# Block 1's feed forward: 28 of 32 inner tiles by seven half-size block products, the state space's tables kept in memory meanwhile

## The chip, the cores and the metric

The kernel runs on one core of a Trainium2 chip. TensorE (PE) does the matrix products; VectorE (DVE), ScalarE (ACT) and GpSimd (POOL) do everything element by element; SyncE (SP) issues most transfers between memory and the core. The metric is device time in microseconds, the median of several runs of the whole program.

## What is computed

Two transformer blocks over 512 tokens of 1024 features in float32. Block 1 is two attention mixers and a feed forward; block 2 is four mixers, one of them a state space (S5), and a gated feed forward. The change touches block 1's feed forward and the tables that block 2's state space reads:

```python
# block 1
hn = rms_norm(h, norm_mlp_pre)
ff = jnp.square(jax.nn.relu(hn @ w_ff1)) @ w_ff2     # 1024 -> 4096 -> 1024
h = h + rms_norm(ff, norm_mlp_post)
# block 2, the state space: these depend on parameters alone
mag = jnp.exp(lr * dt); ab_re = mag * jnp.cos(li * dt); ab_im = mag * jnp.sin(li * dt)
bb_re = cf_re[..., None] * bre - cf_im[..., None] * bim     # and bb_im
# block 2's feed forward
ff = (jax.nn.silu(a @ w_ffn_gate) * (a @ w_ffn_up)) @ w_ffn_down     # 1024 -> 2816 -> 1024
```

## The kernel before

**Products in three parts.** A float32 product is three reduced ones: each operand is split into a high and a low part, and `mm3` (L328 to L330) issues high x high, high x low and low x high into one PSUM bank. `wload` brings 128 x 1024 pieces of weights (`wraw`, three buffers), ScalarE casts the high part (`whi`, L308), VectorE subtracts to get the low part (`wlo`, L309); five buffers of each.

**Block 1's feed forward** (`ffn1`, L1361) makes 32 inner tiles of 128 features by 512 tokens. An inner tile takes 8 x 3 matmuls of 512 columns. `sink` then does relu and square on ScalarE, the square once more on GpSimd (L1375) and the low part on VectorE (L1376); the pair goes into the tag `hid`. `groups` (L1310) takes the tiles in groups of `FF1 = (6, 6, 6, 6, 4, 4)`. After a group's tiles and one tile of the next group (the lead), the group's share of the 4 x 2 outputs (token tile j, half f of the features) is formed in PSUM and added to a tile `y` in SBUF (`Post.part`, L606). The last group's share goes on into the norm (`Post.sink`, `Post.done`). The first five tiles (`HEAD`) of the first group run in half-width pieces (`layer`): three tiles and then two on the first 256 tokens, the two and then the three on the second 256, while the mixer's end still produces the second half of the input.

**The seven products.** Block 2's second matrix ("down") already takes four of its groups by seven products of half-size blocks in place of eight (`seven`, L1270). A group of four inner tiles is two pairs. `Pairs.pair` (L1252) forms, for a pair, two tiles of sums and differences on GpSimd (`sx` and `sy`, four operations of 128 x 256) and splits them, and the tiles themselves, into high and low (tag `g`, 14 buffers a group). `seven` loads four raw weight pieces (`wq`), forms four sums and differences of them on GpSimd (L1291 to L1296), splits seven operands and does seven products, each in two token halves of 2 x 3 matmuls. The products come in the order 1, 2, 7, 6, 4, 5, 3; only the first two need none of GpSimd's pair sums. Each result is added to one of 14 tiles (`Post.seven`, L624; copied the first time, L622). After the last such group `Post.joined` (L627) adds the tiles up to the outputs on GpSimd, 14 additions of 128 x 512.

**The state space's tables** depend on parameters alone and are made inside block 1's feed forward, between groups (the list `between`): `S5.scalars`, then for each half of the channels `S5.maps` in two steps (first many small GpSimd operations on 64 to 128 rows x 64 elements, then TensorE transposes and small products), then `S5.tables`. They fill 16 of the 18 buffers of tag `g` until block 2 reads them.

**Order.** Each engine runs its queue in order. The order in a queue is made when the program is built: by a planner that simulates the engines and takes, whenever an engine comes free, the first instruction in program order that is ready. `issue_after` keeps an instruction behind another of its own engine; `in_order` fixes TensorE's order in some stages.

Of the kernel before, what the change touches and what calls it, by code (L numbers as in the profile page):

```python
# [16 lines left out]
OP = mybir.AluOpType  # L17
# [6 lines left out]
NEG = -1e30  # L24
FF1 = (6, 6, 6, 6, 4, 4)
FF2 = (4, 4, 4, 4, 2, 4)
SEVEN = {"down": range(4)}

# [201 lines left out]
def program(ctx: ExitStack, tc: tile.TileContext, A, out):  # L230
# [227 lines left out]
    class Fill:  # L458


        def __init__(self, lag=1):
            self.plan, self.later = [], [None] * lag
# [765 lines left out]
    class Pairs:  # L1228
# [40 lines left out]

    def seven(nm, g, pairs, post):  # L1270

# [37 lines left out]

    def groups(sizes, tiles, xs, sink, carry, nm, hid, post, nxt, between=(), pairs=None):  # L1310

# [3 lines left out]
        for g, n in enumerate(sizes):  # L1315
            ms = list(range(n0, n0 + n))
            todo = [x for m in ms[lead:] for x in tiles(m)]
            layer(todo, lambda key: [key], xs, sink, first=0 if g else HEAD, carry=carry)
            lead = 1 if g + 1 < len(sizes) else 0
            layer([x for m in range(n0 + n, n0 + n + lead) for x in tiles(m)], lambda key: [key], xs, sink)  # L1320
            if g < len(between):
# [4 lines left out]
            if g in SEVEN.get(nm, ()):  # L1326
                seven(nm, g, pairs, post)
# [33 lines left out]
    def ffn1(carry, old, new, s5):  # L1361

        r2 = cp.tile([128, 4], F32, name="r2f")
        pre = carry[1]
        hid = {}

        def sink(key, ps, ts):
            m = key[1]
            if m not in hid:
                hid[m] = u("hidh", F32R, tag="hid"), u("hidl", F32R, tag="hid")  # L1370
            hi, lo = (t[:, ts] for t in hid[m])
# [6 lines left out]
        def stats():  # L1378
# [7 lines left out]

        po = Post("norm_mlp_post", old, new, "hid")
# [15 lines left out]
    class S5:  # L1403


        def scalars(self):
# [72 lines left out]
        def maps(self, hb):  # L1479
# [4 lines left out]
            VP = [u("vp", tag="s5") for _ in range(2)]  # L1484
            CP = [u("cp", tag="g") for _ in range(2)]
            C0 = u("c0", tag="s5")
# [26 lines left out]
            for c in range(2):  # L1513
                self.CP[c][hb] = CP[c]
            yield
            for c in range(2):
                tp = mps()
                for b in range(4):
                    PE.transpose(tp[:, 128 * b:128 * b + 128], VP[c][:, 128 * b:128 * b + 128], ident)
                self.VM[c][hb] = u("vm", tag="g")  # L1520
                (ACT.copy if c else DVE.tensor_copy)(self.VM[c][hb], tp)

# [17 lines left out]
            DVE.tensor_tensor(kv[:, :, 0:32], kv[:, :, 0:32], dd, op=OP.add)  # L1540
            self.TM[hb] = u("tmx", tag="g")
            POOL.memset(self.TM[hb], 0.0)
            tv = self.TM[hb].rearrange("p (b x) -> p b x", b=4)
            for i in range(4):
                (ACT.copy if i % 2 else DVE.tensor_copy)(tv[32 * i:32 * i + 32, :, 32 * i:128],
                                                         kv[:, :, 0:128 - 32 * i])

        def tables(self):
# [3 lines left out]
            for hb in range(2):  # L1552
                self.RH[hb] = u("rh", tag="g")
                for c in range(2):
                    self.CT[c][hb] = u("ct", tag="g")
                    POOL.memset(f(self.CT[c][hb])[:, :, 0:1], 1.0 - c)
                DVE.tensor_copy(f(self.RH[hb]), self.rho4[:, 4 * hb:4 * hb + 4, None].to_broadcast([128, 4, 128]))
                POOL.memset(f(self.RH[hb])[:, :, 0:1], 0.0)
            other = (self.nx(), self.nx())
            ts = [u("s5u", tag="s5") for _ in range(2)]  # L1560
            for s_ in range(7):
# [6 lines left out]
                if s_ < 6:  # L1568
                    cmul(*other, *cur, *cur, self.scr2, DVE)
                    cur, other = other, cur  # L1570

    def mix2(carry, old, new, s5):
# [800 lines left out]
```

## Time and profile before

| | us |
|---|---|
| median of 3 runs | 1507.68 (1506.07 to 1508.33) |
| the profiled execution | 1511.7 |
| its span, first to last instruction | 1510.0 |
| TensorE busy | 1464.1 (97%) |
| VectorE busy | 866.2 (57%) |
| ScalarE busy | 605.6 (40%) |
| GpSimd busy | 333.0 (22%) |

Block 1's feed forward lies at about 455 to 818 us, block 2's at about 1165 to 1505 us. A busy time is the time in which an engine works on some instruction; matmuls overlap, so TensorE's pace is read from the distance of their starts. In the row of a stretch the columns are: the stretch, its length, the busy time of PE, PEld (weight load), DVE, ACT and POOL with the number of instructions in brackets, the granted TensorE clock (1.00 is full), the busy share of the 16 DMA engines, and GB/s. A timeline row gives start, duration, engine, line, operation, output <- inputs, shape, count, and in square brackets how long the engine was idle before it and who ended that.

### The profile page before, as it was taken

The numbers are of one execution on the slowest core, as the hardware profiler recorded it, in microseconds if no ns is written. First come the engines' busy times: TensorE is split into PE (matmuls) and PEld (weight loads), VectorE is DVE, ScalarE is ACT, GpSimd is POOL, SyncE is SP. The second block draws the span as 40 slices with busy tenths as digits, with TensorE's granted clock in tenths as the row PEclk, the third lists the DMA queues.
The fourth block names the chain that finished last, engine by engine and source line by source line (L and its number), as shares of the span: only waits on it lengthen the run. The fifth ranks groups of instructions, "written<-read, shape, count | busy, mean of one in ns | idle before, by whom it ended". The sixth has DMA issues, their size and how long they took to land. (4 is left out here: it accounts for less than half of the span.)

```text
span 1510.0 us, 21333 instructions
## 1 busy us (share of the span) xinstructions
PE 1464.1 (97%) x8180; PEld 1217.4 (81%) x8184; DVE 866.2 (57%) x1641; ACT 605.6 (40%) x1131; POOL 333.0 (22%) x528
## 2 busy tenths in 40 slices
PE   8999999999999999999998999899998999999997
PEld 6888876688888888888887999667788888888885
DVE  5433368743746534334446686956646657586746
ACT  6344455533335342322325443543525453333322
POOL 0210110000201467203600052411000323134600
PEclk9999999999999999999999999978999999999999
DMA  8332121123234332322334424001115242341322
GB/s 294 117 112 79 57 65 43 43 84 98 96 103 150 119 112 61 122 84 84 112 99 137 150 87 118 30 29 42 43 58 194 84 143 81 98 129 39 139 85 84
DMA packets 54725, 147.32 MB, mean 98 GB/s; under 512 B 9824, under 2 KB 16368, under 8 KB 54624
## 3 DMA queue, kind: packets, MB, share of 16 engines
q1 hardware_dynamic: 52384, 143.38, 29.2%
q10 hardware_dynamic: 1776, 1.85, 0.4%
q8 instruction: 64, 1.05, 0.3%
q0 software_dynamic: 464, 0.74, 0.2%
q14 instruction: 37, 0.30, 0.1%
HBM read 135.12 MB, written 11.06 MB: 97 GB/s over the span
## 5 line engine op out<-in xcount | busy, mean ns | idle before, releaser
L308 ACT CAST whi<-wraw 128x1024 fp32r<-128x1024 f32 (+4 forms) x221 | 217.4, 989 | 381.2 <-PE acc L329 188.2
L309 DVE TENSOR_TENSOR wlo<-wraw,whi 128x1024 fp32r<-128x1024 f32 (+4 forms) x221 | 269.4, 1225 | 160.4 <-ACT whi L308 152.3
L328 PE MATMUL acc<-xh,whi 128*128 128x512 f32 (+1 forms) x920 | 347.9, 379 | 7.5 <-ACT whi L308 5.6
L330 PE MATMUL acc<-xh,wlo 128*128 128x512 f32 (+1 forms) x920 | 343.6, 374 | 1.9 <-DVE wlo L309 1.9
L329 PE MATMUL acc<-xl,whi 128*128 128x512 f32 (+1 forms) x920 | 344.1, 374 | 0.3 <-DVE xl L703 0.3
L328 PEld LDWEIGHTS acc<-xh,whi 128*128 128x128 f32 x920 | 174.2, 189 | 44.2 <-ACT whi L308 7.9
L330 PEld LDWEIGHTS acc<-xh,wlo 128*128 128x128 f32 x920 | 174.1, 189 | 33.8 <-DVE wlo L309 2.7
L329 PEld LDWEIGHTS acc<-xl,whi 128*128 128x128 f32 x920 | 174.3, 189 | 31.6 <-issue 1.0
L328 PE MATMUL acc<-whi,hidh 128*128 128x512 f32 x304 | 119.6, 395 | 0.0
L329 PE MATMUL acc<-wlo,hidh 128*128 128x512 f32 x304 | 119.2, 394 | 0.0
L330 PE MATMUL acc<-whi,hidl 128*128 128x512 f32 x304 | 118.9, 394 | 0.0
L328 PE MATMUL acc<-whi,xh 128*128 128x256 f32 (+3 forms) x352 | 114.5, 325 | 0.2 <-ACT mv L1902 0.2
L329 PE MATMUL acc<-wlo,xh 128*128 128x256 f32 (+3 forms) x352 | 111.7, 317 | 0.0
L330 PE MATMUL acc<-whi,xl 128*128 128x256 f32 (+3 forms) x352 | 111.6, 317 | 0.0
L1375 POOL TENSOR_TENSOR relu<-relu 128x512 f32<-128x512 f32 (+1 forms) x37 | 36.8, 1002 | 230.8 <-ACT hidh L1374 226.7
L328 PEld LDWEIGHTS acc<-whi,xh 128*128 128x128 f32 x352 | 68.3, 194 | 6.9 <-issue 2.2
L330 PEld LDWEIGHTS acc<-whi,xl 128*128 128x128 f32 x352 | 68.0, 193 | 3.9
L329 PEld LDWEIGHTS acc<-wlo,xh 128*128 128x128 f32 x352 | 68.2, 194 | 3.5
L329 PEld LDWEIGHTS acc<-wlo,hidh 128*128 128x128 f32 x304 | 57.2, 188 | 13.2
L330 PEld LDWEIGHTS acc<-whi,hidl 128*128 128x128 f32 x304 | 57.2, 188 | 13.2
L328 PEld LDWEIGHTS acc<-whi,hidh 128*128 128x128 f32 x304 | 57.2, 188 | 13.0
L1284 ACT CAST whi<-wq 128x1024 fp32r<-128x1024 f32 x28 | 29.5, 1055 | 62.1 <-PE acc L329 44.9
(582 smaller groups left out, 2572.0 us busy)
## 6 DMA issues: line engine op xcount, KB each, us to landing
wraw<-in_wp_dram SPq DMA_DIRECT2D x195, 512.0 KB, 3.6
wq<-in_wp_dram SPq DMA_DIRECT2D x16, 512.0 KB, 3.5
hd<-y SPq DMA_DIRECT2D x24, 256.0 KB, 4.4
hr<-hd SPq DMA_DIRECT2D x12, 512.0 KB, 4.5
hr<-in_xt_dram SPq DMA_DIRECT2D x8, 512.0 KB, 5.3
H<-in_xT_dram SPq DMA_DIRECT2D x8, 256.0 KB, 5.2
wraw<-in_wp_dram SPq DMA_DIRECT2D x16, 128.0 KB, 3.9
gain<-in_gv_dram SPq DMA_DIRECT2D x8, 256.0 KB, 4.4
```

The lines of the kernel that those rows point to most:

```text
L308: ACT.copy(hi[:, s], raw[:, s])
L309: eng.tensor_tensor(lo[:, s], raw[:, s], hi.bitcast(F32)[:, s], op=OP.subtract)
L328: PE.matmul(ps, lhsT=w[0], rhs=x[0], start=first, stop=False)
L329: PE.matmul(ps, lhsT=w[0], rhs=x[1], start=False, stop=False)
L330: PE.matmul(ps, lhsT=w[1], rhs=x[0], start=False, stop=last)
L1284: ACT.copy(hi, raw)
L1375: POOL.tensor_tensor(a, a, a, op=OP.mult)
```

## The change

Block 1's feed forward takes groups of four tiles, eight of them; the first seven reach the outputs by seven products. `sink` hands the squared tiles of these groups to `Pairs`; only the last group's four keep the old way. The sums and differences of the weight pieces run on VectorE here (`eng`), in block 2 still on GpSimd. The lead tile is formed in the same call of `layer` as the group, so the first five tiles are the first group and its lead. `sx` and `sy` get two buffers of their own. The buffers of tag `g` now hold the pairs' operands, so the state space's matrices and tables are built in tag `s5`, written to memory (`keep`) and read back into tag `g` by `load` in the last group. The steps of the state space are spread over the groups 0 to 5.

```diff
-FF1 = (6, 6, 6, 6, 4, 4)
+FF1 = (4,) * 8
-SEVEN = {"down": range(4)}
+SEVEN = {"ff2": range(7), "down": range(4)}
...
-            x, y = u("sx"), u("sy")
+            x, y = u("sx", tag="sx"), u("sy", tag="sx")
...
-            POOL.tensor_tensor(t, B1, t, op=OP.subtract)
+            eng.tensor_tensor(t, B1, t, op=OP.subtract)
             yield 7, parts(t)
-            POOL.tensor_tensor(t, t, A0, op=OP.add)
+            eng.tensor_tensor(t, t, A0, op=OP.add)
             yield 6, parts(t)
-            POOL.tensor_tensor(B0, B0, t, op=OP.subtract)
-            POOL.tensor_tensor(t, B1, t, op=OP.subtract)
+            eng.tensor_tensor(B0, B0, t, op=OP.subtract)
+            eng.tensor_tensor(t, B1, t, op=OP.subtract)
...
             todo = [x for m in ms[lead:] for x in tiles(m)]
+            lead = 1 if g + 1 < len(sizes) else 0
+            todo += [x for m in range(n0 + n, n0 + n + lead) for x in tiles(m)]
             layer(todo, lambda key: [key], xs, sink, first=0 if g else HEAD, carry=carry)
-            lead = 1 if g + 1 < len(sizes) else 0
-            layer([x for m in range(n0 + n, n0 + n + lead) for x in tiles(m)], lambda key: [key], xs, sink)
...
+            if m in pairs.of:
+                if m not in rel:
+                    rel[m] = u("relu")
+                a = rel[m][:, ts]
+                ACT.activation(a, ps, AF.Relu)
+                ACT.activation(a, a, AF.Square)
+                pairs.add(m, rel[m], ts)
+                return
...
-               [lambda: (stats(), step(maps[0])()), step(*maps), step(maps[1]), s5.tables])
+               [stats, step(maps[0]), step(maps[0]), step(maps[1]), step(maps[1]), s5.tables, lambda: None, s5.load],
+               pairs, DVE)
...
+        def keep(self, nm, c, hb, t):
+            d = self.kept[nm, c, hb] = dram.tile([128, 512], F32, name=f"k{nm}{c}{hb}")
+            nc.sync.dma_start(out=d, in_=t)
+        def load(self):
+            for hb in range(2):
+                for nm, to in (("vm", self.VM), ("ct", self.CT), ("rh", self.RH)):
+                    for c in range(2 if nm != "rh" else 1):
+                        self.back(nm, c, hb, to)
...
+        def back(self, nm, c, hb, to):
+            t = u(nm, tag="g")
+            nc.sync.dma_start(out=t, in_=self.kept[nm, c, hb])
...
-    with phase("f1", u=3, hid=14, s5=6):
+    with phase("f1", u=5, sx=2, s5=9):
...
-    with phase("f2", u=8):
+    with phase("f2", u=6, sx=2):
```

## Rows read from the trace of the kernel before

**Rows 1.** The page's first part: busy us of each engine.
```profile
PE 1464.1 (97%) x8180; PEld 1217.4 (81%) x8184; DVE 866.2 (57%) x1641; ACT 605.6 (40%) x1131; POOL 333.0 (22%) x528
```

**Rows 2.** Stretches, columns as told above: two of block 1, two of block 2.
```profile
780.00:800.00 20.00, 20.00 (x89) 16.46 (x88) 7.59 (x8) 8.31 (x11) 2.08 (x2) 1.00 0.33 107
820.00:840.00 20.00, 16.85 (x125) 15.00 (x122) 17.55 (x57) 11.74 (x28) 3.44 (x16) 1.00 0.74 243
1265.00:1285.00 20.00, 20.00 (x90) 16.57 (x89) 20.00 (x21) 8.53 (x11) 8.04 (x4) 1.00 0.48 147
```

**Rows 3.** Timeline of PE: end of half-width pieces; first and last of seven matmuls.
```profile
488.60 0.28 PE L330 MATMUL ops<-xh,wlo 128*128 128x256 f32 x1
...
1212.05 0.39 PE L330 MATMUL ops<-whi,prl 128*128 128x512 f32 x1
...
1213.41 0.39 PE L330 MATMUL ops<-whi,prl 128*128 128x512 f32 x1
```

**Rows 4.** Groups by line: count, busy us, mean ns, then idle us before them.
```profile
L309 DVE TENSOR_TENSOR wlo<-wraw,whi 128x1024 fp32r<-128x1024 f32 x195 | 255.2, 1311 | 155.4 <-ACT whi L308 147.3 <-PE mps L1519 5.0 <-DMA wraw<-in_wp_dram 0.8
...
L1285 DVE TENSOR_TENSOR wlo<-wq,whi 128x1024 fp32r<-128x1024 f32 x28 | 50.6, 1807 | 4.4 <-PE ops L330 2.4 <-ACT whi L1284 1.9
...
L624 DVE TENSOR_TENSOR y<-acc,y 128x512 f32<-128x512 f32 x24 | 15.4, 677 | 0.0
```

**Rows 5.** Timeline of DVE, from block 1's and block 2's feed forward.
```profile
583.99 1.23 DVE L309 TENSOR_TENSOR wlo<-wraw,whi 128x1024 fp32r<-128x1024 f32 x1 [1.79 <-ACT whi L308]
...
1360.79 0.69 DVE L2334 TENSOR_TENSOR sil<-sil,acc 128x512 f32<-128x512 f32 x1 [3.42 <-PE acc L330]
...
1366.62 0.69 DVE L336 TENSOR_TENSOR prl<-sy,prh 128x512 fp32r<-128x512 f32 x1
...
1373.65 0.42 DVE L1263 TENSOR_TENSOR a0l<-sil,a0h 128x256 fp32r<-128x256 f32 x1
...
1413.01 1.28 DVE L624 TENSOR_TENSOR y<-acc,y 128x512 f32<-128x512 f32 x2
```

**Rows 6.** Timeline of ACT, end of block 1's half-width pieces; one copy of block 2.
```profile
489.04 0.38 ACT L1373 ACTIVATE relu<-acc 128x256 f32<-128x256 f32 x1
...
491.74 1.04 ACT L1374 ACTIVATE hidh<-relu 128x256 fp32r<-128x256 f32 x3
...
1215.58 0.42 ACT L1262 CAST a0h<-sil 128x256 fp32r<-128x256 f32 x1
```

**Rows 7.** Timeline of POOL, first and last of a pair's four operations.
```profile
1361.55 0.74 POOL L1255 TENSOR_TENSOR sx<-sil 128x256 f32<-128x256 f32 x1 [14.41 <-DVE sil L2334]
...
1365.20 0.74 POOL L1258 TENSOR_TENSOR sy<-sil,sx 128x256 f32<-128x256 f32 x1
```

**Rows 8.** Timeline of POOL, second block of matrices and the tables, firsts and lasts.
```profile
569.01 0.29 POOL L1396 TENSOR_TENSOR s5t<-s5s,s5b 128x64 f32<-128x64 f32 x1
...
584.20 1.17 POOL L1396 TENSOR_TENSOR s5t<-s5s,s5b 128x64 f32<-128x64 f32 x1
...
605.50 0.54 POOL L1494 TENSOR_SCALAR cp<-s5t 64x64 f32<-64x64 f32 x2
...
707.47 0.14 POOL L1556 MEMSET ct<- 128x4 f32 x2
...
743.24 0.74 POOL L1401 TENSOR_TENSOR ct<-s5u 128x256 f32<-128x256 f32 x1
```

**Rows 9.** Timeline of POOL, inside the first block of matrices.
```profile
547.82 1.04 POOL L1375 TENSOR_TENSOR relu<-relu 128x512 f32<-128x512 f32 x1
548.82 0.29 POOL L1399 TENSOR_TENSOR s5t<-s5s,p 128x64 f32<-128x64 f32 x1
```

**Rows 10.** Timeline of POOL, first and last of the 14 additions.
```profile
1406.05 3.53 POOL L629 TENSOR_TENSOR hr<-hr,y 128x512 f32<-128x512 f32 x2 [9.36 <-DVE hr L624]
...
1428.94 1.31 POOL L629 TENSOR_TENSOR y<-y,p 128x512 f32<-128x512 f32 x1
```

**Rows 11.** DMA issues of the page: KB each, us to landing.
```profile
wraw<-in_wp_dram SPq DMA_DIRECT2D x195, 512.0 KB, 3.6
```

More of the change, by code (lines that the diff above doesn't have):

```diff
@@ L1268, in pair, with seven @@
             self.mark = self.mark or last(mybir.EngineType.Activation)
-    def seven(nm, g, pairs, post):
+    def seven(nm, g, pairs, post, eng):
         W = {}
@@ L1308, in seven, with groups @@
                 post.seven(g, i, j, ps)
-    def groups(sizes, tiles, xs, sink, carry, nm, hid, post, nxt, between=(), pairs=None):
+    def groups(sizes, tiles, xs, sink, carry, nm, hid, post, nxt, between=(), pairs=None,
+               eng=POOL):
         n0 = 0
@@ L1326, in groups @@
             if g in SEVEN.get(nm, ()):
-                seven(nm, g, pairs, post)
+                seven(nm, g, pairs, post, eng)
                 if g + 1 not in SEVEN[nm]:
@@ L1364, in ffn1 @@
         pre = carry[1]
-        hid = {}
+        hid, rel = {}, {}
         def sink(key, ps, ts):
             m = key[1]
+            if m in pairs.of:
[6 more added lines that the diff above has]
+                return
             if m not in hid:
-                hid[m] = u("hidh", F32R, tag="hid"), u("hidl", F32R, tag="hid")
+                hid[m] = u("hidh", F32R, tag="g"), u("hidl", F32R, tag="g")
             hi, lo = (t[:, ts] for t in hid[m])
@@ L1385, in ffn1 @@
         step = lambda *ms: lambda: [next(m, None) for m in ms]
-        po = Post("norm_mlp_post", old, new, "hid")
+        po, pairs = Post("norm_mlp_post", old, new, "u"), Pairs("ff2", FF1)
         nxt = Pre("ln_mix_pre_2")
         groups(FF1, lambda m: [("ff1", m)], pre.xs, sink, carry, "ff2", hid, po, nxt,
-               [lambda: (stats(), step(maps[0])()), step(*maps), step(maps[1]), s5.tables])
+               [stats, step(maps[0]), step(maps[0]), step(maps[1]), step(maps[1]), s5.tables, lambda: None, s5.load],
+               pairs, DVE)
         return po, nxt
@@ L1403, in program, with __init__ @@
     class S5:
+        def __init__(self):
+            self.kept = {}
+        def keep(self, nm, c, hb, t):
[6 more added lines that the diff above has]
+                        self.back(nm, c, hb, to)
+            for hb in range(2):
+                for nm, to in (("tm", self.TM), ("cp", self.CP)):
+                    for c in range(2 if nm != "tm" else 1):
+                        self.back(nm, c, hb, to)
+        def back(self, nm, c, hb, to):
+            t = u(nm, tag="g")
+            nc.sync.dma_start(out=t, in_=self.kept[nm, c, hb])
+            if nm in ("rh", "tm"):
+                to[hb] = t
+            else:
+                to[c][hb] = t
         def scalars(self):
@@ L1484, in maps @@
             VP = [u("vp", tag="s5") for _ in range(2)]
-            CP = [u("cp", tag="g") for _ in range(2)]
+            CP = [u("cp", tag="s5") for _ in range(2)]
             C0 = u("c0", tag="s5")
@@ L1513, in maps @@
             for c in range(2):
-                self.CP[c][hb] = CP[c]
+                self.keep("cp", c, hb, CP[c])
             yield
@@ L1519, in maps @@
                     PE.transpose(tp[:, 128 * b:128 * b + 128], VP[c][:, 128 * b:128 * b + 128], ident)
-                self.VM[c][hb] = u("vm", tag="g")
-                (ACT.copy if c else DVE.tensor_copy)(self.VM[c][hb], tp)
+                vm = u("vm", tag="s5")
+                (ACT.copy if c else DVE.tensor_copy)(vm, tp)
+                self.keep("vm", c, hb, vm)
             kp_ = mps()
@@ L1540, in maps @@
             DVE.tensor_tensor(kv[:, :, 0:32], kv[:, :, 0:32], dd, op=OP.add)
-            self.TM[hb] = u("tmx", tag="g")
-            POOL.memset(self.TM[hb], 0.0)
-            tv = self.TM[hb].rearrange("p (b x) -> p b x", b=4)
+            tm = u("tmx", tag="s5")
+            POOL.memset(tm, 0.0)
+            tv = tm.rearrange("p (b x) -> p b x", b=4)
             for i in range(4):
@@ L1546, in maps @@
                                                          kv[:, :, 0:128 - 32 * i])
+            self.keep("tm", 0, hb, tm)
         def tables(self):
@@ L1552, in tables @@
             for hb in range(2):
-                self.RH[hb] = u("rh", tag="g")
+                self.RH[hb] = u("rh", tag="s5")
                 for c in range(2):
-                    self.CT[c][hb] = u("ct", tag="g")
+                    self.CT[c][hb] = u("ct", tag="s5")
                     POOL.memset(f(self.CT[c][hb])[:, :, 0:1], 1.0 - c)
@@ L1558, in tables @@
                 POOL.memset(f(self.RH[hb])[:, :, 0:1], 0.0)
+                self.keep("rh", 0, hb, self.RH[hb])
             other = (self.nx(), self.nx())
@@ L1570, in tables @@
                     cur, other = other, cur
+            for hb in range(2):
+                for c in range(2):
+                    self.keep("ct", c, hb, self.CT[c][hb])
     def mix2(carry, old, new, s5):
```

## The prediction

> **What bounds the kernel now.** I read the busy times first. TensorE is busy for 97% of the span, the next engine, VectorE, for 57%, and GpSimd for 22% [rows 1]. The average hides stages with other limits, so the stretches come next. In block 1's feed forward (about 455 to 818 us) TensorE is busy for all 20.00 us of a slice at a granted clock of 1.00, the higher of its two levels (2.4 GHz), while VectorE needs 7.6 us of the 20. In a seven-product stage of block 2's feed forward VectorE is busy for 20.00 of 20 as well, and TensorE still has no gap [rows 2]. So here time is the number of matmuls times their pace, as long as the other engines keep ahead. The pace: seven starts of full matmuls lie 1.36 us apart in six steps, 0.2267 us each [rows 3]. "Mean 0.39" in a PE row is latency, not pace.
>
> **What is removed.** A group of four inner tiles reached the outputs by 4 tiles x 8 halves of token tiles x 3 = 96 matmuls of 512 columns. By seven products it takes 7 x 2 x 2 x 3 = 84. Seven groups save 7 x 12 = 84 matmuls, 84 x 0.2267 = 19.0 us. The first layer, the last group of four and all of the state space's matmuls keep their number. Regrouping from 6 to 4 tiles adds no matmul.
>
> **What is added, group by group.** A group now lasts (96 + 84) x 0.2267 = 40.8 us. VectorE's work in it: eleven low parts of weights (4 + 7) at 1.31 = 14.4; four sums and differences of weights of the same size and operands, at the same 1.31 = 5.2; 14 evictions at 0.68 = 9.5 (8 before) [rows 4]; the low parts of two pairs, 2 x (3 x 0.69 + 0.42) = 5.0 [rows 5]. Sum 34.1 of 40.8 us: beside TensorE, with a sixth to spare. If the low parts cost the 1.81 of the block 2 row instead of 1.31, it is 7 x 0.5 = 3.5 more, 37.6: still beside. I take nothing for it, and keep 1 us a group, 7 in all, as the upper end, since an eviction also waits behind one such operation of 1.3 us. The spare time is what hides it; where GpSimd holds VectorE up it goes first. ScalarE's casts (11 x 1.05), pair copies, relus and squares stay under 25 us a group: nothing.
>
> **Group 0 loses its cover.** The first five tiles run in half-width pieces, and tiles 0, 1 and 2 end last, together. Before, tile 5 followed at once. Now the products follow, and they need relu and square of three tiles. In the trace these run from 489.04 to 492.78 behind the last matmul of the pieces at 488.6 [rows 3, 6]. Then the first product wants two copies of 0.42 us [rows 6] and a low part of 0.42 [rows 5]: it starts about 5 us late, and the third needs GpSimd's pair sums, 4.4 us a pair [rows 7], which the first two products (5.4 us) hide in part. Tile 5 can fill some of the time once its weights are in; the five buffers of split weights are partly taken by the products' own. I take 4.5 us lost; ends 0 (all filled) and 8 (nothing filled and the third product late).
>
> **Groups 1 to 6.** One tile of the next group (24 x 0.2267 = 5.4 us) lies between the last tile and the products; block 2 has two there. From the finished second tile of a pair to its last low part block 2 takes 1361.48 to 1367.31, 5.8 us, when GpSimd has no weight sums to do [rows 5, 7]. With relu and square (1.3 us) it is 7.1; the third product, the first that needs GpSimd, starts 5.4 + 5.4 = 10.9 us after the tile. So it is hidden with 3.8 us to spare.
>
> **GpSimd's queue.** The state space's matrices are two blocks of small operations, 37.0 us each (569.01 to 606.04), the tables one of 36.5 [rows 8]. Each now begins behind a group's pair sums and runs into the next group's. GpSimd runs in order, so what counts is where the pair sums stand in its queue. In the old block the square of a relu stands before a step of a complex product (L1399), not behind the block [rows 9]: the queue lets in what is ready wherever a step waits for the one before. With the same order a pair's four operations pass in some 4 x (0.75 + 0.9) = 6.6 us beside the block, against 4.4 alone [rows 7]: 2.2 us later, inside the 3.8. But the matrices' small matmuls wait for the block's end one group (40.8 us) later, formerly 65. I take 0.5 us for each of three blocks, 1.5; ends 0 and 22 (the rival below).
>
> On two engines at one memory the row shows this: an operation of the block that takes 0.29 us [rows 9] takes 1.17 [rows 8] where it meets a low part of weights that began 0.2 us before [rows 5]. The Trainium skill ("SBUF — State Buffer", "Who interferes with whom") has it as an exclusive lock: a VectorE instruction with two SBUF inputs and a GpSimd instruction that reads SBUF shut each other out for their whole length. The trace agrees, 0.9 us lost a time; by that rule moving the weight sums to VectorE takes GpSimd's time after all, and the sum would go towards the slower rival.
>
> **The end.** The last group's three squares on GpSimd stand behind the 14 additions that join the products. In block 2 these run from 1406.05 to 1430.24, 16 us past the last eviction [rows 5, 10]. Three tiles take 3 x 5.4 = 16.3 us, so the low parts of tiles 29 to 31 come just late: 1 us (0 to 4). The tables' way to memory and back is 2 x 16 x 256 KB = 8.4 MB, of which the stretches in question, at a DMA share of 0.33 [rows 2], have room. The copies out wait on SyncE's queue for GpSimd, and the weights' loads stand behind them; a load takes 3.6 us [rows 11], and three raw and five split buffers lie ahead. The last six loads (1.5 MB) wait for the last hidden tiles and fall into the change to block 2, where the DMA share is 0.74 at 243 GB/s already [rows 2]: 1.5 / 0.243 = 6 us of transfer, mostly not in front of anything TensorE waits for. 1 us for both (0 to 6). Block 2's smaller pools: its pairs are 10 us and more apart, nothing (0 to 1).
>
> **Sum.** -19.0 + 4.5 + 1.5 + 1 + 1 + 0.5 (VectorE somewhere) = -10.5 us. The profiled execution took 1511.7 us (1.7 more than its span), 4.0 above the median 1507.68 of the runs shown; 1511.7 - 10.5 = 1501.2 there, 1497.2 on the median's scale.
>
> **Rivals.**
> *GpSimd's queue becomes the bound (slower).* Place: the third product of groups 2, 4 and 6. If the pair sums stand behind the blocks: a block is 37.0 us with six meetings of about 0.9 us like that one, 31 without [rows 5, 8, 9]. In a group VectorE now has 15 such long operations, 15 x 0.9 = 13.5, and half as much a time for six short ones, 3: 31 + 16.5 + two pairs of 3.0 alone = 53.5, and 1.3 for cast and low part, 54.8 us after the products begin. The third product of the next group is due at 40.8 + 5.4 = 46.2 (with the small matmuls 48). 6.5 to 8.5 lost, three times: 22 instead of 1.5, so +10: 1517.7. It decides from about 6 us lost a block. For it: the lock. Against it: the order in [rows 9], and a sixth of VectorE's time free.
> *All covers hold.* Tile 5 fills the first gap and nothing is late: -19 + 1 = -18, 1489.7. For it: block 2's stages, with VectorE full and no gap [rows 2]; against: the first group's chain.
> *VectorE becomes the bound.* 34.1 us counts no waiting. At the 1.81 us of block 2's low parts for all 15 long operations [rows 4] it is 34.1 + 7.5 = 41.6, and with evictions late behind them 2 us a group over 40.8: 14 lost beside the 4.5 and the rest, -19 + 14 + 4.5 + 2 = +1.5: 1509. For it: 20.00 of 20 busy in block 2; against: there GpSimd's weight sums do the blocking, and these are gone here.
> That fewer products are formed than said is excluded: each group's operands come from its own four tiles, and nothing else reaches the outputs.
>
> **From these to the numbers.** Forecast (-6 to -15) 0.50; all covers 0.17; VectorE 0.13; GpSimd's queue 0.20. A measurement of this kernel can tell 0.2%, 3 us. Faster: 0.50 + 0.17 + a third of VectorE's 0.13 = 0.71; same 0.12 (the rest of VectorE's, a little of the queue's); slower 0.17. The range reaches from the middle of the full covers, 1489, to just past VectorE's case, 1511, and leaves out most of the queue's case and half of the best.
>
> **What would show it.** 84 fewer matmuls of 512 columns; a gap of 4 to 5 us on PE behind the first five tiles; PE full in the slices of groups 1 to 6, VectorE at 16 to 18 of 20 us; the pair sums standing among the state space's small operations. Wrong: PE gaps of over 3 us before the products of groups 2, 4 or 6 with GpSimd's sums as releaser, gaps behind low parts or evictions, or a gap at the change to block 2 that is longer than before.

## The result, and the profile after

The changed kernel takes 1529.88 us against 1508.01 for the kernel before on the same chip, both medians of four executions: a ratio of 1.0133 [1.0106, 1.0161], slower by 1.3%. One of the changed kernel's four was slow (1634.87 us, at a mean granted clock of 0.84) and counts neither in the ratio nor in the differences below, which start from the median of the other three, 1528.79 (1526.79 to 1530.96). The forecast was 1497.2 us, with a range of 1489 to 1511. Its profiled execution took 1526.79 us, 15.1 more than that of before.

The page's busy times, which answer to [rows 1]:

```profile
PE 1450.2 (95%) x8100; PEld 1202.8 (79%) x8100; DVE 977.5 (64%) x1765; ACT 656.9 (43%) x1214; POOL 396.4 (26%) x565
```

TensorE does less work and is idle for longer. In block 1's feed forward the trace has 1699 matmuls before and 1615 after, 84 fewer, as forecast. The stretch begins at 465.36 us before and 465.87 after, and the last matmul ahead of the same wait at its end starts at 826.47 and 842.23: all of the loss is here. So 84 x 0.2267 = 19.0 us were won, and some 34 lost again. The stretches, the first three against [rows 2], and two more of the changed kernel (columns as there). They are the same times, not the same instructions: behind block 1's feed forward the changed kernel is 15 us later in its work.

```profile
780.00:800.00 20.00, 20.00 (x81) 16.23 (x82) 17.37 (x22) 8.14 (x9) 13.88 (x8) 0.91 0.32 107
820.00:840.00 20.00, 17.29 (x83) 13.79 (x82) 15.73 (x36) 10.50 (x27) 1.18 (x3) 1.00 0.85 293
1265.00:1285.00 20.00, 20.00 (x90) 16.57 (x89) 13.28 (x11) 7.28 (x10) 10.74 (x7) 1.00 0.09 27
540.00:560.00 20.00, 12.14 (x54) 9.73 (x52) 16.85 (x22) 6.23 (x7) 18.06 (x39) 0.88 0.56 184
640.00:660.00 20.00, 14.63 (x59) 11.61 (x58) 13.06 (x16) 5.16 (x5) 17.47 (x47) 0.83 0.41 131
```

VectorE went from 7.6 to 17.4 of 20 us at 780 to 800. TensorE is busy for all 20 us there too, but at a mean granted clock of 0.91, with 81 matmuls in place of 89. It is idle for 8 and 5 us in the last two rows, where GpSimd is the busiest engine. What TensorE waited for in the whole stretch (sum, times, longest):

```profile
PE mps L1555 <- POOL vp L1530: 14.3, 2, 8.9
PE ops L328 <- ACT prh L335: 4.5, 2, 4.0
PE mps L697 <- DVE y L664: 2.4, 4, 0.9
PE acc L328 <- ACT prh L335: 2.2, 3, 1.4
PE acc L330 <- DVE hidl L1385: 2.1, 1, 2.1
```

L1555 holds the transposes of the state space's matrices, L1530 the paddings that write them. The places, from the timeline of PE (the bracket is the idle time before, and what ended it):

```profile
494.81 0.73 PE L330 MATMUL acc<-whi,prl 128*128 128x512 f32 x2 [1.37 <-DVE prl L336]
...
501.68 0.50 PE L328 MATMUL acc<-whi,prh 128*128 128x512 f32 x1 [1.38 <-ACT prh L335]
...
551.75 0.39 PE L330 MATMUL acc<-whi,prl 128*128 128x512 f32 x1
561.04 1.50 PE L1555 MATMUL mps<-cstt,vp 128*128 128x128 f32 x5 [8.90 <-POOL vp L1530]
...
652.66 2.14 PE L1555 MATMUL mps<-cstt,vp 128*128 128x128 f32 x8 [5.37 <-POOL vp L1530]
...
779.87 0.50 PE L328 MATMUL ops<-whi,prh 128*128 128x512 f32 x1 [4.00 <-ACT prh L335]
...
814.36 0.61 PE L330 MATMUL acc<-whi,hidl 128*128 128x512 f32 x1 [2.10 <-DVE hidl L1385]
```

In TensorE's order the transposes stand ahead of the last 12 matmuls of group 1's products (the second time ahead of the last 18 of group 3's) and of the next group's tiles. The tiles depend on nothing in GpSimd, yet they wait. The timeline of POOL, which answers to [rows 8 to 10]:

```profile
538.13 0.40 POOL L1406 TENSOR_TENSOR s5b<-s5s,p 128x128 f32<-128x128 f32 x1 [0.51 <-DVE s5s L1497]
...
555.73 1.27 POOL L1409 TENSOR_TENSOR s5t<-s5s,s5b 128x64 f32<-128x64 f32 x1
556.97 0.29 POOL L1410 TENSOR_TENSOR s5t<-s5s,s5b 128x64 f32<-128x64 f32 x1
...
560.42 0.56 POOL L1530 TENSOR_SCALAR vp<-s5t 64x64 f32<-64x64 f32 x2
...
576.89 0.54 POOL L1530 TENSOR_SCALAR cp<-s5t 64x64 f32<-64x64 f32 x2
577.52 0.73 POOL L1255 TENSOR_TENSOR sx<-relu 128x256 f32<-128x256 f32 x1
...
774.55 0.74 POOL L1255 TENSOR_TENSOR sx<-relu 128x256 f32<-128x256 f32 x1
...
787.08 2.21 POOL L629 TENSOR_TENSOR hr<-hr,y 128x512 f32<-128x512 f32 x1 [5.61 <-DVE hr L624]
...
810.69 3.06 POOL L1384 TENSOR_TENSOR relu<-relu 128x512 f32<-128x512 f32 x3
```

The first block of matrices runs from 538.13 to 577.43, 39.3 us, nearly a whole group of 40.8; TensorE asks for its first half at 552.1. The sums of group 2's first pair (L1255) come behind its last padding: the slipping in of [rows 9] did not happen here. It did beside the tables, but the last pair there came at 774.55, and the product waited 4.00 us.

### The profile page after: what moved, and what is told of

It reads as the page before. It is cut to its first block, busy times and chain, and to the rows that moved or that the text cites. A ratio compares the mean times of both kernels' runs of the same rounds, so it can differ in the third digit from the quotient of the medians.

```text
span 1525.1 us, 21495 instructions
## 1 busy us (share of the span) xinstructions
PE 1450.2 (95%) x8100; PEld 1202.8 (79%) x8100; DVE 977.5 (64%) x1765; ACT 656.9 (43%) x1214; POOL 396.4 (26%) x565
## 4 chain that ended last, share of the span: by engine, by line
PE 73%; DVE 11%; POOL 8%; ACT 3%; DMA 2%; issue 2%; SPq 0%; DVEq 0%; ACTq 0%; POOLq 0%
PE acc L328 20%; PE acc L330 19%; PE acc L329 19%; DVE wlo L309 1%; PE acc L1127 1%; DMA wraw<-in_wp_dram 1%; PE ops L330 1%; ACT junk L671 1%; PE ops L328 1%; PE ops L329 1%; PE ops L1067 1%; PE ops L1157 1%; POOL y L629 1%; DVE wlo L1285 1%; POOL vp L1530 1%
## 5 line engine op out<-in xcount | busy, mean ns | idle before, releaser
L308 ACT CAST whi<-wraw 128x1024 fp32r<-128x1024 f32 (+4 forms) x193 | 187.9, 980 | 261.9 <-PE acc L329 101.3
L309 DVE TENSOR_TENSOR wlo<-wraw,whi 128x1024 fp32r<-128x1024 f32 (+4 forms) x193 | 233.9, 1218 | 68.4 <-ACT whi L308 65.8
L1284 ACT CAST whi<-wq 128x1024 fp32r<-128x1024 f32 x77 | 80.9, 1051 | 133.6 <-PE acc L329 75.5
L1285 DVE TENSOR_TENSOR wlo<-wq,whi 128x1024 fp32r<-128x1024 f32 x77 | 113.0, 1468 | 34.1 <-ACT whi L1284 31.7
L328 PE MATMUL acc<-whi,prh 128*128 128x512 f32 x220 | 88.3, 402 | 4.0 <-ACT prh L335 2.2
L330 PE MATMUL acc<-whi,prl 128*128 128x512 f32 x220 | 86.1, 395 | 1.4 <-DVE prl L336 1.4
L329 PE MATMUL acc<-wlo,prh 128*128 128x512 f32 x220 | 86.8, 395 | 0.0
L1255 POOL TENSOR_TENSOR sx<-relu 128x256 f32<-128x256 f32 x14 | 14.6, 1045 | 186.4 <-ACT relu L1375 117.1
L821 POOL TENSOR_TENSOR gt<-gt 128x512 f32<-128x512 f32 x8 | 10.4, 1294 | 172.5 <-DVE gt L820 169.9
L328 PEld LDWEIGHTS acc<-whi,prh 128*128 128x128 f32 x220 | 42.3, 193 | 16.1 <-ACT prh L335 3.5
```

The costliest lines, as they stand in the source:

```text
L308: ACT.copy(hi[:, s], raw[:, s])
L309: eng.tensor_tensor(lo[:, s], raw[:, s], hi.bitcast(F32)[:, s], op=OP.subtract)
L328: PE.matmul(ps, lhsT=w[0], rhs=x[0], start=first, stop=False)
L329: PE.matmul(ps, lhsT=w[0], rhs=x[1], start=False, stop=False)
L330: PE.matmul(ps, lhsT=w[1], rhs=x[0], start=False, stop=last)
L1284: ACT.copy(hi, raw)
```

## The experiments

All times of this table are medians of the whole program; the kernel before lay at 1507.4 to 1507.9 in these comparisons, and ratios are to it. Theory A after the two traces: GpSimd's in-order block of matrices, and who stands behind it, costs the 34 us. Rivals: VectorE is the bound; the state space's work costs by its amount; the halves' products bring nothing.

| run | us | ratio | run | us | ratio |
|---|---|---|---|---|---|
| edge | 1525.85 | 1.0120 [1.0103, 1.0137] | padkeep | 1512.39 | 1.0031 [1.0018, 1.0044] |
| nospace | 1487.72 | 0.9877 [0.9852, 0.9901] | padedge | 1513.43 | 1.0033 [1.0022, 1.0044] |
| poolsums | 1545.22 | 1.0248 [1.0233, 1.0263] | comb2 | 1518.06 | 1.0062 [1.0041, 1.0083] |
| lead2 | 1527.04 | 1.0124 [1.0108, 1.0140] | comb3 | 1509.91 | 1.0014 [0.9998, 1.0030] |
| bnos | 1503.75 | 0.9988 [0.9969, 1.0007] | notab | 1513.84 | 1.0041 [1.0027, 1.0055] |
| scal | 1525.81 | 1.0116 [1.0095, 1.0136] | nomat | 1495.62 | 0.9922 [0.9909, 0.9935] |
| padact | 1512.72 | 1.0027 [1.0012, 1.0042] | comb4 | 1506.78 | 1.0000 [0.9990, 1.0011] |
| spread | 1518.87 | 1.0071 [1.0051, 1.0091] | comb5 | 1503.32 | 0.9972 [0.9959, 0.9985] |

The whole program also moves with what lies outside block 1's feed forward, so the length of this stage is read from the traces as well, one trace a run: from the first transposes of the change to it (L697) to the first of the change to block 2. Begin and end in the kernel before, the changed kernel, nospace and bnos, from their timelines of PE:

```profile
449.32 0.60 PE L697 MATMUL mps<-cstt,y 128*128 128x128 f32 x4
817.34 0.33 PE L697 MATMUL mps<-cstt,y 128*128 128x128 f32 x1 [0.19 <-DVE y L664]
```

```profile
449.82 0.60 PE L697 MATMUL mps<-cstt,y 128*128 128x128 f32 x4
833.19 0.30 PE L697 MATMUL mps<-cstt,y 128*128 128x128 f32 x1 [0.36 <-DVE y L664]
```

```profile
451.26 0.60 PE L697 MATMUL mps<-cstt,y 128*128 128x128 f32 x4
798.01 0.30 PE L697 MATMUL mps<-cstt,y 128*128 128x128 f32 x1 [0.36 <-DVE y L664]
```

```profile
449.69 0.60 PE L697 MATMUL mps<-cstt,y 128*128 128x128 f32 x4
807.20 0.30 PE L697 MATMUL mps<-cstt,y 128*128 128x128 f32 x1 [0.36 <-DVE y L664]
```

| | before | changed | nospace | bnos | nomat | notab | edge | padact | spread | comb5 |
|---|---|---|---|---|---|---|---|---|---|---|
| stage, us | 368.0 | 383.4 | 346.7 | 357.5 | 357.1 | 372.8 | 383.6 | 371.1 | 373.3 | 361.7 |

**edge: the transposes behind the group's tiles.**

```
+            tiles_done = last(mybir.EngineType.PE)
             for c in range(2):
...
-                    PE.transpose(tp[:, 128 * b:128 * b + 128], VP[c][:, 128 * b:128 * b + 128], ident)
+                    with tc.issue_after(tiles_done):
+                        PE.transpose(tp[:, 128 * b:128 * b + 128], VP[c][:, 128 * b:128 * b + 128], ident)
```

> The changed kernel, with the eight transposes of each set of matrices put behind the tiles of the group in TensorE's order (108 and 114 matmuls later, 24.5 and 25.8 us at 0.2267 us each). Theory A (TensorE stands in order before transposes whose matrices GpSimd hasn't written): the idle times of 8.90 us at 551.75 and 5.37 us at 646.90 go, and with them the stretches at a lower granted clock behind them (2.0 and 2.5 us), at most 18.8 us; I expect 10 to 18 us off the 1526.8 of the profiled execution, 1509 to 1517. The matrices are ready at 562 and 653.6 and the transposes come at 577 and 672, so no wait is left there. Rival B (VectorE, busy 18 to 19 of 20 us in most stretches, is the bound, and TensorE would wait for something of VectorE's soon after anyway): under 5 us, 1522 or more. Rival C (the one on record: GpSimd's queue makes the third product of groups 2 and 4 wait): the two waits go and waits of 6.5 to 8.5 us for pair sums appear in groups 2 and 4; 1520 to 1526.

1525.85: theory A in that form failed; the time is in C's range, and the waits moved to the operands as C said, though the longest is 4.44 us and not 6.5 to 8.5. The 14.3 us of waits at the transposes are gone, and as much came back: the stage is as long as in the changed kernel, 383.6 against 383.4 us. The timelines of PE and of ACT in edge:

```profile
584.14 0.80 PE L328 MATMUL acc<-whi,a0h 128*128 128x512 f32 x1 [4.44 <-ACT a0h L1262]
...
593.02 0.31 PE L1567 MATMUL mps<-c,vp 128*32 128x32 f32 x4 [1.36 <-DVE vm L1559]
```

```profile
563.86 0.62 ACT L335 CAST prh<-relu 128x512 fp32r<-128x512 f32 x1
580.41 0.62 ACT L335 CAST prh<-sx 128x512 fp32r<-128x512 f32 x1 [15.93 <-POOL sx L1256]
580.93 1.04 ACT L1284 CAST whi<-wq 128x1024 fp32r<-128x1024 f32 x1
```

ScalarE takes no weights and no other operand for 15.93 us, because the cast at the head of its queue wants a pair sum that GpSimd has behind the block. VectorE waits behind ScalarE, and then TensorE. In the changed kernel the same cast waits only 4.50 us, because TensorE's 8.90 us had already held up the work ahead of it:

```profile
579.68 0.62 ACT L335 CAST prh<-sx 128x512 fp32r<-128x512 f32 x1 [4.50 <-POOL sx L1256]
```

**nospace and bnos: neither kernel's state space work in the feed forward.** In both, scalars, matrices and tables are left out and constants stand for the tables. The edit shown is nospace's; bnos has `[stats, lambda: None, lambda: None, s5.consts]`, where `consts` fills the 16 buffers of tag `g` with 0.5.

```
-               [stats, step(maps[0]), step(maps[0]), step(maps[1]), step(maps[1]), s5.tables, lambda: None, s5.load],
+               [stats] + [lambda: None] * 6 + [s5.load],
-            s5.scalars()
-            nc.sync.dma_start(out=t, in_=self.kept[nm, c, hb])
+            POOL.memset(t, 0.5)
```

> The changed kernel without the state space's scalars, matrices and tables in block 1's feed forward, and so without their way through memory; the second half gets constants in place of the tables, so the output is another. Theory A: all waits that the state space makes go: 8.90 + 2.0, 5.37 + 2.5, and 4.00 + 1.6 at 775, together 24.4 us, so about 1502, and group 0 (5.8 us) and the last group's squares (3.5 us) stay as they are. Rival B (VectorE's weight conversions and evictions are the bound whatever GpSimd does): the gain is that of the VectorE instructions left out, some 15 us of busy time beside idle stretches, under 6 us of the end; 1520 or more. The prediction's own sum of 1497 would be missed by some 5 us under A (group 0's 1.3 and the squares' 2.5 over their terms, and 3.2 us at 735 to 747).

> A control: the kernel before without the state space's scalars, matrices and tables (constants in place of the tables, so the output is another). In the changed kernel leaving them out took 38 to 42 us off (1487.7). Theory A (the state space's work hid behind TensorE before the change, and it is the change that uncovered it): the kernel before loses little, 0 to 8 us (some 20 of its matmuls are small ones of the matrices, under 5 us): 1500 to 1508, and the halves' products alone are then worth 12 to 20 us. Rival D (the state space's work costs its 35 us in either kernel, and the halves' products bring nothing): 1470 to 1480.

By the medians the change is worth 1503.75 - 1487.72 = 16.0 us without the state space, and the state space's work costs 1507.37 - 1503.75 = 3.6 us in the kernel before and 1528.79 - 1487.72 = 41.1 in the changed one. By the length of the stage the same three are 357.5 - 346.7 = 10.8, 10.5 and 36.7 us. The medians also hold what is outside: from the end of the stage to block 2's feed forward the trace of bnos takes 327.1 us, that of nospace 319.9, that of the kernel before 316.8, and why is not known. The traces are of single executions, those of nospace and bnos 7.3 and 5.7 us above their medians. So the work's cost rose by some 26 to 38 us. By either measure it is not true that the halves' products bring nothing, and their own load on VectorE does not bound the stage (rows of nospace stand under "Why the prediction was wrong").

Theory A had the kind right and 14 us too little for the median. In the stage its 24.4 us lack the state space's 80 small matmuls (5.5 us by the distances of their starts in the trace of before, where they are paid too) and the 3.2 us at 735 to 747; with these 33 of the 36.7 us have a place.

**poolsums: the weight sums of block 1 on GpSimd.**

```
-               pairs, DVE)
+               pairs, POOL)
```

> The changed kernel with the 28 sums of weights in block 1 on GpSimd (as the last feed forward has them) in place of VectorE: 34 us (28 x 1.22) leave VectorE, 67 to 78 us (28 x 2.4 to 2.8) come onto GpSimd. Theory A (GpSimd's queue sets when the transposes can start): the block operations of the matrices end later and TensorE waits longer; 5 to 25 us slower than the changed kernel, 1532 to 1552. Rival B (VectorE is the bound): faster than the changed kernel by 5 us or more, 1522 or less.

1545.22, 16.4 us over the changed kernel, in A's range: GpSimd's time is what is short, VectorE's is not. The way is another than A's: one wait at the transposes is left, 7.1 us, and TensorE waits 9.3 us in five places for casts of the pairs' operands.

**lead2: two tiles before group 0's products.**

```
-            lead = 1 if g + 1 < len(sizes) else 0
+            lead = 0 if g + 1 == len(sizes) else 2 if g == 0 and nm == 'ff2' else 1
```

> The changed kernel with two tiles of group 1 in place of one before group 0's products (24 matmuls, 5.4 us, more of cover; nothing else moved). If group 0's idle times (0.29, 1.37, 0.50, 0.48 and 1.38 us, with the slow pace between them 5.8 us at 490 to 500) come from operands that aren't split yet, 3 to 5.5 us of them go: 1521 to 1524. If VectorE's throughput in the whole of group 0 is the cause (18.6 of 20 us at 500 to 520), the same time is lost at the third or fourth product instead: 1526 to 1528.

1527.04, in the range of the second reading. Yet group 0's loss at 490 to 520 fell from 5.8 to 3.3 us, so operands that come late are a cause of it. The 2.5 us don't reach the end, because later waits moved: the matrices' small matmuls wait 5.93 us for a copy, and group 2's first product 3.42, in place of the 8.90.

**scal: the scalars before the first group.**

```
+        s5.scalars()
         maps = [s5.maps(hb) for hb in range(2)]
...
             po.scaled(r2)
-            s5.scalars()
```

> The changed kernel with the state space's scalars put ahead of the first group (VectorE has 11 of 25 us busy there) in place of behind its tiles. If the slow scalars (30.6 us on VectorE, 507.5 to 538.1) are what made GpSimd's first block of matrices late, the block starts some 20 us earlier, the wait of 8.90 us and the 2.0 us behind it go: 1514 to 1518. Theory A (the block's place in GpSimd's queue is what counts: behind the pair sums of group 1, which end at 536.5 in the changed kernel): the block starts at 535 to 537, the wait stays at 6 to 9 us, and only VectorE is freer: 1520 to 1528.

1525.81, in theory A's range, with a shorter wait than it gave. In the changed kernel the scalars' chain takes 507.5 to 538.1 on VectorE, but without it the block starts no sooner: its zeroing comes at 541.84 (538.47 in the changed kernel), behind group 1's pair sums. The wait fell from 8.90 to 5.38, and the first transposes of the stage came at 470.34 in place of 465.87, which takes that back.

**padact: the paddings of each block on ScalarE** (36 of them in the trace, not 44 as the expectation has it).

```
-                    POOL.tensor_scalar(d[r, :, i, e, :], src[r], -1.0 if neg else 1.0, 0.0, op0=OP.mult, op1=OP.add)
+                    ACT.activation(d[r, :, i, e, :], src[r], AF.Copy, scale=-1.0 if neg else 1.0)
```

> The changed kernel with the matrices' 44 paddings of each block on ScalarE (busy 43% of the span) in place of GpSimd (0.31 to 0.43 us each, 13 us in each block of 39 us). Theory A (length of GpSimd's block): the blocks end 13 us earlier each, so the transposes' waits of 8.9 and 5.4 us go or fall to under 3 us with the clock behind them: 1508 to 1518, provided that ScalarE's queue, where the paddings now stand before weights and operands, doesn't wait for the products of GpSimd in turn. Rival E (an in-order queue again: ScalarE's weight conversions stand behind paddings that wait for GpSimd): the waits move to whi of the weights, 1524 or more.

1512.72, 16 us under the changed kernel, 12.3 of them in the stage: the largest gain of one line, and the most direct evidence that the length of GpSimd's block is the larger part of the cause. In its timeline of PE the one wait left at the transposes is

```profile
552.04 0.63 PE L1555 MATMUL mps<-cstt,vp 128*128 128x128 f32 x4 [2.88 <-POOL s5t L1410]
```

**spread: the same instructions in smaller portions.** The blocks of matrices are cut in two, the tables after the sixth doubling; with edge and scal.

```
+            yield
             pad(C0, 0, cc[0])
...
-               [stats, step(maps[0]), step(maps[0]), step(maps[1]), step(maps[1]), s5.tables, lambda: None, s5.load],
+               [lambda: (stats(), step(maps[0])()), step(maps[0]), step(*maps), step(maps[1]), step(maps[1], tabs), step(tabs),
+                lambda: None, s5.load],
```

> The changed kernel with the state space's work cut finer: scalars ahead of the first group, each block of matrices in two halves of some 20 us in two groups, its transposes behind the tiles of the next group, the tables in two parts. The number of instructions is the same. Theory A (a block of 39 us on GpSimd's in-order queue, nearly as long as a group's 40.8 us, is what delays both the transposes and the pair sums of the next group): the waits at 552, 647 and 775 (8.9, 5.4, 4.0 us) and the lower clock behind them (2.0, 2.5, 1.6) go but for small ones: 1500 to 1508, between the 1526 of the changed kernel and the 1488 without the state space. Rival F (the state space's work costs by its amount: VectorE's lock with GpSimd, memory, the small matmuls): 1518 or more.

1518.87: 10 us gained. The stage is 10.1 us shorter, and the early scalars push its begin back by 3.8 us (477.2 in place of 473.4 for the last transposes of the change to block 1's feed forward). That is too little for A and inside F's range, by 0.9 us; what comb5 does with the same work below speaks against F. Its longest wait is new, 4.28 us for an eviction at 744: VectorE waits 2.90 us for raw weights. Padkeep tests why.

**padkeep and padedge: one thing each on top of padact.**

```
-            nc.sync.dma_start(out=d, in_=t)
+            nc.gpsimd.dma_start(out=d, in_=t)
```

> As padact (paddings on ScalarE), and the tables' way to memory issued from GpSimd's queue in place of SyncE's. In padact's trace TensorE still loses some 3.3 us at 725 to 732 and 2.8 at 640 to 647 to weights that come late; in spread's VectorE waits 2.90 us at 741 for raw weights whose load stands on SyncE behind a copy that waits for GpSimd's last table. If SyncE's in-order queue is the cause, these go: 1506 to 1510 beside padact's 1512.7. If the transfers themselves (16 engines at 0.3 of their time) or VectorE are: no change, 1511 to 1515.

> As padact, with the transposes behind the tiles of the group (as edge). With GpSimd's block 13 us shorter the pair sums of the next group no longer stand 16 us behind it. If the block's length and the transposes' place are two waits of which the later shows, the 2.88 us at 552 left in padact goes with its slow clock of 1.3 us: 1507 to 1511. If the transposes' place moves the wait to the operands again (as in edge): 1511 to 1515.

1512.39 and 1513.43 beside 1512.72: neither gave anything. In padkeep the weights' wait at 726 is 1.23 us, 1.19 in padact, so SyncE's queue was not its cause; in padedge the wait moved to the operands, as in edge.

**notab and nomat: half of the state space's work each.** Constants stand for what is left out.

```
-               [stats, step(maps[0]), step(maps[0]), step(maps[1]), step(maps[1]), s5.tables, lambda: None, s5.load],
+               [stats, step(maps[0]), step(maps[0]), step(maps[1]), step(maps[1]), lambda: None, lambda: None, s5.load],   # notab
+               [stats] + [lambda: None] * 4 + [s5.tables, lambda: None, s5.load],   # nomat
```

> The changed kernel without the state space's tables (constants in their place; scalars and matrices stay). If the losses add up by place (changed kernel 1526 to 1530, without all of it 1487.7), the tables' share is the 4.00 us at 775 with its clock (1.6 us) and the late weights at 735 to 747 (3.2 us): 7 to 10 us, so 1517 to 1521. If the tables' instructions, not their place, were the cost, half of the 40 us or more would go: 1510 or less.

> The changed kernel without the state space's two sets of matrices and their transposes (constants in their place; scalars and tables stay). Matrices' share by place: 8.90 + 2.0 and 5.37 + 2.5 us, some 4 us of small matmuls on TensorE, and smaller waits: 19 to 28 us, so 1499 to 1509. If the scalars on VectorE are the root instead, under 12 us: 1515 or more.

Without tables 15.0 us less than 1528.79, without matrices 33.2; together 48.1, over the 41.1 of both, and each 3 us outside its expectation by place. In the stage the shares do add: 383.4 - 372.8 = 10.6 for the tables and 383.4 - 357.1 = 26.3 for the matrices, 36.9 beside 36.7 for both, and they are near the 7 to 10 and inside the 19 to 28 that the places gave. The matrices are the larger part. The surplus of the medians lies outside the stage or between executions; its cause is not known.

**comb2, comb3, comb4, comb5: all together.** comb3 is padact, spread, edge, scal and padkeep, with the last group's squares and the matrices' copies moved:

```
-            POOL.tensor_tensor(a, a, a, op=OP.mult)
+            DVE.tensor_tensor(a, a, a, op=OP.mult)
...
-                (ACT.copy if c else DVE.tensor_copy)(vm, tp)
+                ACT.copy(vm, tp)
```

comb2 has lead2 and not the copies; comb4 is comb3 without scal; comb5 is comb4 with the tables cut after the fifth doubling (`if s_ in (4,): yield`).

> All of the changes tried, together: paddings on ScalarE, scalars first, blocks in halves, transposes behind the tiles, the tables' transfers from GpSimd's queue, the last group's squares on VectorE, and two tiles of cover before group 0's products. If the state space's work costs only where an in-order queue makes something wait, what is left is its small matmuls on TensorE (under 4 us) and some waits: 1490 to 1500, faster than the kernel before. If VectorE's load or its lock with GpSimd is a cost by itself: 1503 or more.

> As comb2 without the second tile of cover in group 0, and with the copies of the matrices out of PSUM and into the tables (10 of them 0.3 to 0.7 us) on ScalarE in place of VectorE. If VectorE's queue behind these copies makes evictions late (waits of 3.7 and 4.7 us for L624's in spread): 1490 to 1500, no slower than comb2. If group 0's cover is worth its 2.5 us, comb3 is that much behind comb2.

> comb3 with the scalars back behind the first group's tiles (ahead of the first group they pushed its begin from 473.4 to 479.9 us in comb3). Everything else as comb3: paddings and copies on ScalarE, blocks in halves, transposes behind tiles, the tables' transfers from GpSimd's queue, squares on VectorE. If the 5 to 6 us at the begin come back and the scalars' slow run on VectorE costs nothing in their old place (scal: nothing gained by moving them), 1503 to 1506, faster than the kernel before. If the scalars cost the same there (products of group 0 late): 1508 to 1511.

> comb4 with the tables cut one doubling earlier (19 and 21 us of GpSimd in place of 28 and 13). The wait of 2.8 us at 726 in comb3 (operand of the third product behind the first part) should go; if the second part (21 us) makes the next group's third product wait in turn, the time is that of comb4; else 2 to 4 us less.

Comb2's 1518.06 is in the range of the reading it was to rule out, VectorE's load; at 726 it waits 3.88 us for a relu behind its longer lead. Comb3's 1509.91 missed its range by 10 us, 6 of them at the begin (the same transposes end at 479.9). Putting the scalars back gave 3.1 (comb4), and smaller table parts 3.5 more. Comb5, 1503.32, is faster than both kernels, 4.5 us under the one before. What its TensorE waits for, from the longest sums:

```profile
PE mps L697 <- DVE y L664: 3.8, 6, 0.9
PE acc L328 <- ACT prh L335: 2.2, 3, 1.4
PE acc L330 <- DVE prl L336: 2.1, 2, 1.4
PE acc L328 <- ACT cp L1532: 2.1, 2, 1.9
```

The first row is the change to block 2, as before; the second is mostly group 0; the last is ScalarE, which now holds the paddings. No wait for GpSimd is among them. Its stage is 15.0 us longer than nospace's: 5.8 of waits, 5.5 of the state space's small matmuls, and 3.7 of other matmuls at a larger distance.

## Why the prediction was wrong

**The step that failed is "GpSimd's queue": 1.5 us, 0.5 for each of three blocks.** Two of its sentences did not hold.

"But the matrices' small matmuls wait for the block's end one group (40.8 us) later, formerly 65." The transposes come 14 us after the block's begin, at 552.1, and they need its first 23 us of 39.3, not its end. I read the distance from the code, where the second step is called one group later. The order of TensorE's instructions is planned, and in it the transposes went ahead of the last of group 1's products and of the next group's tiles. What binds is who stands behind the waiting instruction in its queue; for TensorE that was everything.

"The queue lets in what is ready wherever a step waits for the one before." [Rows 9] showed one square let in. The first pair's sums of groups 2 and 4 stood behind the whole block. The forecast had 2.2 us of delay against 3.8 to spare; edge shows 15.93 at ScalarE.

Taken together the runs without the state space put the term at 36.7 - 10.5 = 26.2 us in the stage and 41.1 - 3.6 = 37.5 by the medians, in place of 1.5. It was bounded at 22 from above, from one mechanism at one kind of place.

**The rival "GpSimd's queue becomes the bound"** named the right engine, at a chance of 0.20. Its place was wrong: the third product waited for it once, 4.00 us in group 6, and not in groups 2 and 4, where the transposes had waited first. Its price for a block under the lock was too high (47.5 us, the 53.5 without the two pairs; 39.3 measured; its loss a block is 6.8 to 8.6 us by its own numbers, not 6.5 to 8.5), and the slower outcome came all the same. The row behind that price is there again (1.27 us against 0.29 in the timeline of POOL above).

**The rival "VectorE becomes the bound"** is ruled out. Its low parts of `wq` cost less than the 1.81 of [rows 4] where GpSimd has no weight sums (in poolsums, which has them, the 49 of block 1 take 1.51 us each); groups by line, mean ns of one after the bar:

```profile
L309 DVE TENSOR_TENSOR wlo<-wraw,whi 128x1024 fp32r<-128x1024 f32 x167 | 219.8, 1318 | 63.6 <-ACT whi L308 61.1
...
L1285 DVE TENSOR_TENSOR wlo<-wq,whi 128x1024 fp32r<-128x1024 f32 x77 | 113.0, 1468 | 34.1 <-ACT whi L1284 31.7 <-PE ops L330 2.4
...
L624 DVE TENSOR_TENSOR y<-acc,y 128x512 f32<-128x512 f32 x72 | 46.7, 677 | 9.7 <-PE acc L330 9.7
```

The 77 of L1285 include block 2's 28; with those at the 50.6 us of [rows 4] the 49 of block 1 take 1.27 us each. In nospace VectorE is busy for 11 to 19 of 20 us in the slices from 520 to 760, and TensorE for all 20.00 of each, without a wait. So block 1's groups can run at their 40.8 us without the state space. Two of these slices:

```profile
540.00:560.00 20.00, 20.00 (x90) 16.56 (x89) 19.37 (x25) 8.97 (x11) 0.00 (x0) 1.00 0.55 175
560.00:580.00 20.00, 20.00 (x90) 16.54 (x89) 11.17 (x13) 10.27 (x16) 7.73 (x8) 1.00 0.11 37
```

**What held.** Matmuls: -19.0, 84 fewer. Group 0: 5.8 lost, 4.5 forecast. The last squares behind the 14 additions: 2.10 us and 1.7 of lower clock after it, 3.8 against 1, inside 0 to 4. The change to block 2: as long as before (5.7 us lost in both), so the last six loads cost nothing there; at 735 to 747 another 3.2 us went to late weights (one wait of 1.20 us) and to evictions, against 1 for both. The forecast's sum without the 1.5 for GpSimd's queue is -12.0 us. Without the state space the traces give -19.0 + 5.8 for group 0 + some 2 for the last squares = -11.2, and -10.8 as the difference of the stages (-16.0 by the medians). So the forecast of the products alone was right, to some 1 us in the stage.

## What to carry to other kernels

A cover is the distance between two instructions in the queues as they are issued, not in the code: ask, for each in-order queue, what stands behind the one that waits. A wait taken away at one queue shows what the next had hidden (edge: 14.3 us of waits removed, the stage as long as before), so cost a block of side work by leaving it out of both kernels, and compare the stage as well as the whole program. When the period of the main work shrinks from 65 to 41 us, side work in blocks of 39 has to be cut or moved to an engine with time to spare; here that, with the squares and copies moved, was worth 1528.79 - 1503.32 = 25.5 of the 41 us.

## What the runs showed of the hardware

In these traces a wait of 2 us or more at TensorE cost more than its length. After the idle 8.90 us the granted clock was at 0.50, the lower of its levels (1.2 GHz), for some 4 us, and so after 5.37; after 4.00 and 2.10 it was at 0.57 and 0.54 on the mean of the first stretch. Behind group 0's short waits (1.38 us the longest) it stayed at 1.00 in the changed kernel. It did not in the trace of nospace: there the waits of the same place, 1.37 us the longest, were followed by 0.53. So these traces give no length of a wait below which the clock stays. Stretches of the changed kernel, PEclk third from the end:

```profile
490.00:515.00 25.00, 20.96 (x86) 15.42 (x85) 22.42 (x30) 19.05 (x36) 11.37 (x8) 1.00 0.39 119
...
552.00:561.00 9.00, 0.14 (x1) 0.00 (x0) 4.85 (x6) 1.04 (x1) 7.96 (x20) 0.68 0.57 190
561.00:565.00 4.00, 3.96 (x13) 3.26 (x14) 0.99 (x2) 0.00 (x0) 3.24 (x13) 0.50 0.20 72
565.00:570.00 5.00, 5.00 (x22) 4.06 (x22) 2.60 (x3) 1.05 (x1) 4.36 (x13) 0.96 0.00 0
...
653.00:657.00 4.00, 4.00 (x14) 3.20 (x13) 0.00 (x0) 0.00 (x0) 3.22 (x14) 0.50 0.04 16
...
780.00:784.00 4.00, 4.00 (x11) 3.17 (x12) 4.00 (x7) 2.24 (x3) 1.04 (x1) 0.57 0.01 3
...
814.40:817.00 2.60, 2.60 (x7) 2.02 (x8) 2.60 (x3) 0.00 (x0) 0.00 (x0) 0.54 0.32 48
```

The one of nospace:

```profile
498.60:502.00 3.40, 3.40 (x9) 2.32 (x9) 3.40 (x3) 1.41 (x3) 2.63 (x3) 0.53 0.08 23
```

Set against 0.2267 us a matmul (and 0.109 a transpose, their distance in the trace of edge), the starts behind the changed kernel's four waits lose another 2.3, 2.6, 1.7 and 1.7 us: a quarter to four fifths of the wait again, which the forecast had not priced. Even padact's 2.88 us at 552 is followed by 1.8.
